# A two-layer token mixer with experts: modulations per 128 columns, rows and weight loads around the second layer's gather, gate-row products of a tile pair in one group

## The chip, the cores and the metric

One core of a Trainium2 chip runs the kernel. The metric is device time in microseconds of one execution; the three runs shown took 2120.23, 2123.27 and 2123.53 us, median 2123.27.

## What is computed

A backbone of two layers works on 512 latent tokens and 256 context tokens of width 1024, all in float32. Each layer normalises the rows, scales and shifts them by modulations (six vectors of 1024 per layer, made by a product of a condition vector with a 1024 x 6144 matrix), mixes the tokens, adds the result, normalises again and sends the rows through 16 experts. The first layer's mixer joins gated linear attention and a gated linear recurrence; the second is a bidirectional matrix memory. Cut to what matters here:

```python
mods = split(silu(c) @ mod_w[layer] + mod_b[layer], 6)        # sh1 sc1 g1 sh2 sc2 g2
xn = rmsnorm(x, norm1_g[layer]) * (1 + sc1) + sh1
y = mixer(xn)                  # layer 0: xn @ ab_w_in (2592 columns), scans, @ ab_w_out
                               # layer 1: xn @ m_w_up (4096 columns), q/k/v, gates, memory, @ m_w_down
x = x + g1 * y
t = rmsnorm(x, norm2_g[layer]) * (1 + sc2) + sh2
probs = softmax(t @ router_w[layer])
gate, idx = top_k(probs.T, 2 * tokens // 16)                  # each expert chooses its tokens
xe = t[idx]
ye = (silu(xe @ w_gate) * (xe @ w_up)) @ w_down * gate
x = x + g2 * scatter_add(idx, ye)
gates(d) = concat(q, k, v) @ w_gates[d] + b_gates[d]          # layer 1: 16 rows of gates in all
```

Every expert has three 1024 x 1024 matrices, so each layer's experts read 16 x 12 MB of weights.

## The kernel before, in words

The program is written as Python that emits instructions; the framework's planner then sets the order of the instructions on each engine by a simulated timeline. Three means bind it: program order, which gives the priority; a raised priority for the splitting of weights (`high_priority`, line 338); and `issue_after(x)`, which queues the instructions of a block behind `x` on the same engine. TensorE, VectorE, ScalarE, GpSimd (POOL) and SyncE (SP) each work through their own queue in order.

**Weights and slots.** Weights come in pieces of 1 MB into slots of 8 KB per partition (`slot`, line 79), which are handed out in a fixed cycle; a load waits until its slot's last reader is done. In the first layer's mixer the cycle has four slots, and both the weights of the projections (`load_cols`, line 101) and those of the modulations (`load_rows`, line 114) take them in program order, so that each load stands four places behind the one whose slot it takes. All of these loads are issued from SyncE's queue.

**Projections.** `proj_tiles` (line 365) loads 256 columns of a weight, and yields the product for each 128 of them (`proj`: the weights are split into a high and a low part, and 48 products of each 128 columns are added in one PSUM tile). After each 256 columns it calls `fill_step` (line 217).

**Modulations.** `mod_block` (line 172) is a generator for one block of 1024 columns in two halves. A half loads two slots, makes the products with 32 columns of the condition (line 182, four row groups at 32-partition offsets), copies the result, and yields; the next call transposes it back by small products (line 190), adds the bias (line 193) and goes on with the next half. `fill_step` takes one such step. The first layer's list (line 411) has six blocks, so twelve steps with products and a thirteenth that only finishes. Steps run at the places where `fill_step` is called: in `proj_tiles`, and twice behind each of the two column halves of the value projection (lines 460 to 482). What is left over runs at line 522, ahead of a branch (line 528) that chooses between two forms of the linear attention, at which the engines meet. In the second layer the list holds steps made on VectorE (`mod_steps`, line 225).

**The second layer's up projection.** For each 128 columns, `up_tile` (line 1481) makes a convolution, a block-diagonal product and `gx`, two 128 x 32 factors. For each pair of such tiles the gate rows are made by four products per column range (lines 1523 to 1530): two factors times the tile before its convolution or after it, each into its own 32 partitions of a PSUM tile, for 512 latent and 256 context columns; VectorE adds the sum to `gacc`.

**The way into the second layer's experts.** After the memory, `down` (line 1563) makes the down projection in two halves of 512 columns; the first half's result is multiplied by the modulation `G` and added to the residual (lines 1608 to 1614). `route_end` (line 1075) scales the rows and writes them to memory for the gather (lines 1105 to 1108, buffers `xt`, written by GpSimd's queue to `xh_d`), finds each expert's tokens by eight rounds of maxima, and writes the indices `gidx` (line 1158). `experts` (line 1166) then gathers the first expert's rows (`fetch`, line 1183, an indirect DMA on GpSimd's queue), transposes them (line 1207), and makes for each expert the gate, up and down products (line 1252).

Weights for the first two experts are sent ahead (lines 1278 to 1280): 22 slots in the pools `r1` (3), `r2` (6), the ring (4), `r3` (7) and `ry` (2), in the order gate weights of expert 0, all from its third up piece on, and at last its first two up pieces (`first`, line 1632). The first three loads are queued behind marks in the memory, the others behind a load of the down projection, all on SyncE. The pool `r3` lies where the memory's tiles were, `ry` where the routing's tiles are (`Br`, freed by the writes of `xh_d`). From the second expert on, each load takes the slot of a weight that has been used.

Of the kernel before, what the change touches and what calls it, by code (L numbers as in the profile page):

```python
# [9 lines left out]
F32 = mybir.dt.float32  # L10
# [5 lines left out]
ALU = mybir.AluOpType  # L16
# [4 lines left out]
P = 128  # L21
D = 1024
# [26 lines left out]
class Backbone:  # L49
# [81 lines left out]
    def setup(self):  # L131
        nc, cp, I = self.nc, self.cp, self.I
        self.cols = cp.tile([P, NCOL], F32, name="cols")
        nc.scalar.dma_start(self.cols, I["cols"])
        self.ident = cp.tile([P, P], F32, name="ident")
        make_identity(nc, self.ident)

        self.sT = cp.tile([P, 8, 32], F32, name="sT")
        nc.vector.memset(self.sT, 0.0)
        for v, nme in enumerate(("c", "c_ctx")):  # L140
            nc.scalar.activation(self.sT[:, :, v], self.col(nme, 0, 8), AF.Silu)

        self.modc = cp.tile([P, 2, 6, 8, 2], F32, name="modc")
        self.g_d = self.dr.tile([2, 2, 8, 2, P], F32, name="g_d")
        self.mhalf = cp.tile([P, 1], F32, name="mhalf")
        nc.vector.memset(self.mhalf, -0.5)
        self.one = cp.tile([P, 1], F32, name="one")
        nc.vector.memset(self.one, 1.0)

        self.pick = cp.tile([P, 2], F32, name="pick")  # L150
        nc.vector.tensor_reduce(
            self.pick, self.ident.rearrange("p (g r) -> p r g", g=4)[:, :2, :], AX.X, ALU.add
        )

        self.copy = cp.tile([P, 2], F32, name="copy")
        for v, n in enumerate((2, 4)):
            for i in range(n):
                nc.vector.memset(self.copy[i * (P // n) : (i + 1) * (P // n), v : v + 1], float(i))
        self.fill = []
        self.eps = cp.tile([P, 1], F32, name="eps")  # L160
        nc.vector.memset(self.eps, EPS)
        self.gla_limit = GLA_LIMIT
        E = mybir.EngineType
        self.flag_engines = [E.PE, E.Activation, E.DVE, E.Pool]
        self.rw = cp.tile([P, 2, KC, NE], F32, name="rw")
        nc.scalar.dma_start(self.rw, I["rw"])
        self.xh_d = [self.dr.tile([n, D], F32, name=f"xh{v}_d") for v, n in enumerate((TL, TC))]
        self.xa_d = [self.dr.tile([n, D], F32, name=f"xa{v}_d") for v, n in enumerate((TL, TC))]
        self.ss = cp.tile([P, NT, 2], F32, name="ss")
# [195 lines left out]
    def proj_tiles(self, pool, w2d, c0, n, ctx=True):  # L365

        for c in range(c0, c0 + n, 256):
            w = self.load_cols(w2d, c, min(256, c0 + n - c))
            for j in range(0, min(256, c0 + n - c), P):
                yield self.proj(pool, w[:, :, j : j + P], P, ctx)  # L370
            self.fill_step()

    def apply_T(self, lhs, rhs, M=P):

# [6 lines left out]
    def layer0(self):  # L381
        tc, nc, I = self.tc, self.nc, self.I
# [11 lines left out]
        with ExitStack() as sx:  # L394
            px = op("A_x", sx)
# [47 lines left out]
        with ExitStack() as sr:  # L443
            prg = op("A_rg", sr)
            bd = prg.tile([P, 8, P], F32, name="bd")
            nc.gpsimd.memset(bd, 0.0)
            xb = [xb_[:, j, :] for j in range(4)]
            for j, pw in enumerate(self.proj_tiles(big, w_in, 2080, 512)):
                xr = prg.tile([P, T], F32, tag="rt", name=self.nm("xr"), bufs=4)
                nc.scalar.copy(xr, pw[:, TC:])  # L450
                self.conv(xb[j], xr, "rg_cw", 4, j, "rg_cb")
            self.rg_pair(prg, 0, xb, bd, sps, h)
            nc.vector.tensor_copy(lr, self.proj32(self.load_cols(w_in, 1536, 32))[:, TC:])
            for j, pw in enumerate(self.proj_tiles(big, w_in, 0, 256)):
                nc.scalar.mul(q[:, j, :], pw[:, TC:], 0.125)
            for j, pw in enumerate(self.proj_tiles(big, w_in, 256, 256)):
                nc.scalar.copy(k[:, j, :], pw[:, TC:])
            last = self.rg_pair(prg, 1, xb, bd, sps, h)

            for c in range(2):  # L460
                w = self.load_cols(w_in, 512 + 256 * c, 256)
                wp = []
                for hf in range(2):
                    wp.append([big.tile([P, 4, 256], F32R, tag=t_, name=self.nm("wv"), bufs=2) for t_ in ("wh", "wl")])
                    with tc.high_priority(offset=HP):
                        self.split(*wp[hf], w[:, 4 * hf : 4 * hf + 4, :], True)
                pw = [self.pW() for _ in range(2)]
                acc = [pw[t // 2][:, 512 * (t % 2) : 512 * (t % 2) + 256] for t in range(4)]
                acc += [self.pT()[:, :256] for _ in range(2)]
                for hf in range(2):  # L470
                    for t in range(NT):
                        i, x0 = (1, t) if t < 2 else (0, t - 2)
                        for kk in range(4 * hf, 4 * hf + 4):
                            wh, wl = (a[:, kk % 4, :] for a in wp[hf])
                            for n, (a, b) in enumerate(((self.xh, wh), (self.xh, wl), (self.xl, wh))):
                                nc.tensor.matmul(
                                    acc[t], a[i][:, kk, ts(x0, P)], b, start=kk == 0 and n == 0, stop=kk == KC - 1 and n == 2
                                )
                        if hf:
                            nc.scalar.copy(v[:, t, ts(c, 256)], acc[t])  # L480
                self.fill_step()
                self.fill_step()
        o = big.tile([P, 4, T], F32, tag="o", name="o_gla")
        with ExitStack() as sg:
            pg = op("A_gla", sg)
# [156 lines left out]
        sb = ExitStack()  # L642
# [432 lines left out]
    def route_end(self, R, small, mid=None):  # L1075
# [27 lines left out]
        last = nc.scalar.activation(pr, pr, AF.Exp)  # L1103
        with self.tc.issue_after(last.ins):
            for t in range(t0, t0 + nt):
                xt = pool.tile([P, D], F32, tag="xt", name=self.nm("xt"), bufs=2)
                nc.scalar.mul(xt, self.xt(t), rs[:, t - t0 : t - t0 + 1])
                nc.gpsimd.dma_start(self.xh_d[v][ts(t - t0, P), :], xt)
        nc.vector.tensor_reduce(sm, pr, AX.X, ALU.add)
# [56 lines left out]
    def experts(self, layer, has_ctx, px, queued=None, once=None):  # L1166
# [66 lines left out]
        def load(n, eng=None):  # L1233
            e, n = divmod(n, 12)
            return self.load_pairs(W[n // 4][e], 256 * (n % 4), eng)
# [39 lines left out]
        if has_ctx:  # L1275
            queue = [(5, nc.sync, None), (8, nc.gpsimd, self.fetched[0]), (12, nc.gpsimd, self.fetched[1])]
        else:
            for n, l in enumerate(once[1]):
                with self.tc.issue_after((self.marks + [queued] * 22)[n].ins):
                    ahead[l] = load(l)  # L1280
            self.set_ring(*once[2])
            queue = []
        xeT = expand(xe, regions[:1])
# [140 lines left out]
    def layer1(self):  # L1424
# [93 lines left out]
        for j, pu in enumerate(up):  # L1518
            pr.append((j, *up_tile(pu, j)))
            if j % 2 == 0:  # L1520
                continue

            for c0, n in ((TC, TL), (0, TC)):
                pg = self.pT()
                for g in range(4):
                    jj, xm, gx = pr[g // 2]
                    src = xm[:, c0 : c0 + n] if g % 2 else (xc, xk)[c0 == 0][jj]
                    nc.tensor.matmul(
                        pg[32 * g : 32 * g + 32, :n], gx[:, g % 2, :], src, start=True, stop=True
                    )  # L1530
                if j == 1:
                    nc.vector.tensor_copy(gacc[:, c0 : c0 + n], pg[:, :n])
                else:
                    nc.vector.tensor_tensor(gacc[:, c0 : c0 + n], gacc[:, c0 : c0 + n], pg[:, :n], ALU.add)
            pr = []
# [60 lines left out]
        with tc.tile_pool(name="C_dn", bufs=1, side="right", reuse_waits="tile") as pd:  # L1596
            G = self.mod_rows(pd, 1, 2, 1)
            for nh in range(2):
# [8 lines left out]
                        queued = self.loaded  # L1607
                for t in range(4):
                    xs = self.xt(2 + t)[:, ts(nh, 512)]
                    y = acc[t]  # L1610
                    if nh == 0:
                        y = pd.tile([P, 512], F32, tag="y", name=self.nm("y"), bufs=2)
                        nc.vector.tensor_tensor(y, acc[t], G[:, 0, :512], ALU.mult)
                    nc.vector.tensor_tensor(xs, xs, y, ALU.add)
                if nh == 0:
                    w = [self.pW(), self.pW()]
                    R = self.route_open(1, 0, pr, w[0][:, :512])
# [6 lines left out]
        self.psum_moe()  # L1624
        sr.close()
        sb = ExitStack()
        r3 = self.weight_ring(sb, 7, "right")
        px = self.pool(self.sb, "Bx", 2, "left")
        sy = ExitStack()
        ry = self.weight_ring(sy, 2, "left")  # L1630
        self.set_ring(r1, r2, self.ring, r3, ry)
        first = [*range(4), *range(6, 22), 4, 5]
        self.experts(1, False, px, queued, (sy, first, (r1, r2, self.ring, r3)))
        sy.close()
        self.moe_close()
        s2.close()
# [358 lines left out]
```

## Time and profile before

| | |
|---|---|
| median of 3 runs | 2123.27 us |
| profiled execution | 2123.27 us |
| its span, first to last instruction | 2121.6 us |
| mean granted TensorE clock | 0.976 |
| TensorE matmul busy | 1974.9 us (93%) |
| VectorE busy | 881.8 us (42%) |
| ScalarE busy | 570.6 us (27%) |
| GpSimd busy | 234.9 us (11%) |
| bytes moved | 587.06 MB, mean 277 GB/s |

The stages follow each other: the first layer's mixer until about 360 us, its output projection and routing until 470, its experts until 1030, the second layer's up projection until 1300, the memory until 1540, down projection and routing until 1645, and the second layer's experts to the end. The shares of busy time are means over these stages and say little of any one of them. A granted clock of 1.00 is 2.4 GHz, 0.50 is 1.2 GHz.

### The profile page before, as it was taken

The page shows a single profiled execution, that of the slowest core. Times are in us where ns is not written, and L with a number is a line of the kernel's source. Part 1 is how long each engine was busy: PE and PEld are TensorE (multiplying, and loading weights), DVE is VectorE, ACT ScalarE, POOL GpSimd, SP SyncE. Part 2 cuts the span into 40 slices and gives each one's busy share as a digit, 9 for nine tenths or more (in the row PEclk, how much of TensorE's full clock was granted, in tenths as well). Part 3 has the DMA queues.
Part 4 walks back from the last instruction along what each step waited for, and adds up shares of the span by engine and source line. Part 5 has one row for each costly group of instructions (what it writes and reads, how often), then busy time and mean ns, then how long its engine had stood idle before and what let it go on. Part 6 is the DMA issues. An engine that isn't in the chain of part 4 may idle for free. (4 is left out here: it accounts for less than half of the span.)

```text
span 2121.6 us, 30206 instructions
## 1 busy us (share of the span) xinstructions
PE 1974.9 (93%) x12346; PEld 1180.4 (56%) x12346; DVE 881.8 (42%) x1765; ACT 570.6 (27%) x1009; POOL 234.9 (11%) x286
## 2 busy tenths in 40 slices
PE   6998997989999999999999999999996799998886
PEld 4676775763444444444678867888875233333322
DVE  3654673561101111021777766467675132222223
ACT  3365442520000000011533435455433000000001
POOL 1000100211111111110000012311140000000000
PEclk8998997999999999999999999999998899999999
DMA  8443523548999999999455555433846899999997
GB/s 303 131 143 100 181 82 103 200 172 326 411 403 404 410 401 411 404 414 377 148 180 183 186 180 166 158 124 110 292 194 238 307 419 420 420 420 419 420 420 289
DMA packets 188303, 587.06 MB, mean 277 GB/s; under 512 B 15304, under 2 KB 84984, under 8 KB 139008
## 3 DMA queue, kind: packets, MB, share of 16 engines
q1 hardware_dynamic: 172816, 546.50, 66.7%
q0 software_dynamic: 11168, 33.46, 4.9%
q10 hardware_dynamic: 4176, 5.11, 0.7%
q8 instruction: 100, 1.64, 0.3%
q14 instruction: 43, 0.35, 0.0%
HBM read 544.60 MB, written 40.42 MB: 276 GB/s over the span
## 5 line engine op out<-in xcount | busy, mean ns | idle before, releaser
L1252 PE MATMUL L<-w,xeT 128*64 128x512 f32 x2048 | 476.1, 600 | 21.4 <-DMA w<-in_exp_w_gate_dram 10.8
L1252 PEld LDWEIGHTS L<-w,xeT 128*64 128x64 f32 x2048 | 145.0, 137 | 322.8 <-issue 261.9
L1252 PE MATMUL L<-w,hL 128*64 128x512 f32 x1024 | 228.3, 596 | 16.7 <-ACT hL L1328 11.8
L1309 DVE TENSOR_TENSOR sgl<-sgl,L 128x512 f32<-128x512 f32 x32 | 22.0, 689 | 365.1 <-PE L L1252 364.3
L1252 PEld LDWEIGHTS L<-w,hL 128*64 128x64 f32 x1024 | 70.0, 137 | 152.0 <-issue 121.1
L1265 PE MATMUL C<-w,xeT 128*32 128x256 f32 x2048 | 116.9, 380 | 1.3 <-DVE xeT L1214 1.3
L1303 ACT ACTIVATE sgl<-L 128x512 f32<-128x512 f32 x32 | 19.1, 598 | 347.6 <-PE L L1252 347.6
L1328 ACT COPY hL<-T 128x512 f32<-128x512 f32 x32 | 18.8, 586 | 335.0 <-PE T L1326 335.0
L276 DVE TENSOR_TENSOR wl<-w,wh 128x1024 fp32r<-128x1024 f32 (+1 forms) x80 | 86.6, 1084 | 40.1 <-ACT wh L274 39.5
L345 PE MATMUL W<-xhl,wl 128*128 128x512 f32 x256 | 102.0, 398 | 1.3 <-DVE wl L276 1.3
L345 PE MATMUL W<-xhl,wh 128*128 128x512 f32 x256 | 103.0, 402 | 0.0
L345 PE MATMUL W<-xll,wh 128*128 128x512 f32 x256 | 101.7, 397 | 0.0
L1183 POOL DMA_INDIRECT xe<-xh_d,gidxL x32 | 31.5, 984 | 633.5 <-PE T L1207 629.6
L1265 PEld LDWEIGHTS C<-w,xeT 128*32 128x32 f32 x2048 | 64.2, 110 | 63.6 <-issue 25.8
L345 PE MATMUL W<-x,wh 128*128 128x512 f32 x256 | 96.4, 399 | 0.6 <-ACT y L324 0.6
L1419 DVE TENSOR_TENSOR X<-X,T 128x512 f32<-128x512 f32 x76 | 48.0, 683 | 95.4 <-PE T L1417 95.3
L274 ACT CAST wh<-w 128x1024 fp32r<-128x1024 f32 (+1 forms) x64 | 53.1, 831 | 112.0 <-PE W L347 71.4
L347 PE MATMUL W<-x,wh 128*128 128x256 f32 x256 | 72.2, 282 | 0.0
L1369 DVE SCALAR_TENSOR_TENSOR y<-L,gateL,G 64x512 f32<-64x512 f32 x32 | 24.0, 750 | 115.3 <-PE L L1252 114.8
L1840 PE MATMUL T<-w,Ah 128*128 128x512 f32 x192 | 62.1, 401 | 1.4 <-ACT Ah L274 1.4
L1372 ACT CAST yL<-y 64x512 fp32r<-64x512 f32 x36 | 22.2, 617 | 150.5 <-DVE y L1369 134.6
L1265 PE MATMUL C<-w,hC 128*32 128x256 f32 x1024 | 58.6, 380 | 0.0
(514 smaller groups left out, 3580.4 us busy)
## 6 DMA issues: line engine op xcount, KB each, us to landing
w<-in_exp_w_gate_dram SPq DMA_DIRECT2D x128, 1024.0 KB, 20.5
w<-in_exp_w_up_dram SPq DMA_DIRECT2D x125, 1024.0 KB, 20.1
w<-in_exp_w_down_dram SPq DMA_DIRECT2D x124, 1024.0 KB, 20.1
w<-in_mod_w_dram SPq DMA_DIRECT2D x48, 1024.0 KB, 5.6
w<-in_m_w_up_dram SPq DMA_DIRECT2D x16, 1024.0 KB, 5.9
w<-in_ab_w_in_dram SPq DMA_DIRECT2D x10, 1024.0 KB, 5.2
w<-in_m_w_down_dram SPq DMA_DIRECT2D x8, 1024.0 KB, 10.0
vh_d<-vth SPq DMA_DIRECT2D x16, 384.0 KB, 3.0
```

The source lines that it names most:

```text
L274: i = (nc.vector.tensor_copy if vector else nc.scalar.copy)(hi, src)
L276: return i, nc.vector.tensor_tensor(lo, src, hi.bitcast(F32), ALU.subtract)
L345: nc.tensor.matmul(pw[:M, 512:], a[:, k, :M], b[0][:, k, :], **st)
L347: nc.tensor.matmul(pw[:M, 256:512], a[:, k, :M], b[1][:, k, :], **st)
L1183: self.fetched.append(nc.gpsimd.indirect_dma_start(out=xe[v], out_offset=None, in_=self.xh_d[v][:, :].rearrange("t (h c) -> (t h) c", c=w) ...
L1252: last = nc.tensor.matmul(L[64 * h : 64 * h + 64, :], a, w[k_ // 2][:, k_ % 2, ts(h, 512)], start=k_ == 0, stop=k_ == KC - 1,)
L1265: last = nc.tensor.matmul(C[32 * h : 32 * h + 32, :], b, w[k_ // 2][:, k_ % 2, ts(h, 256)], start=k_ == 0, stop=k_ == KC - 1,)
L1309: nc.vector.tensor_tensor(sgl, sgl, ul, ALU.mult)
L1369: nc.vector.scalar_tensor_tensor(y32[ph, :], dl[ph, :], gL[ph, e : e + 1], G[ph, 0, ts(h, 512)], ALU.mult, ALU.mult)
L1372: nc.scalar.copy(hi, y32[ph, :])
L1419: nc.vector.tensor_tensor(xs, xs, ps, ALU.add)
L1840: nc.tensor.matmul(O, x_[:, s, :], y_[s], start=s == 0 and m == 0, stop=s == NT - 1 and m == 2)
```

## The change

1. In the first layer, `fill_step` is called after every 128 columns instead of every 256, until the second recurrence pair has been emitted (`often`); behind each half of the value projection one step is left instead of two.
2. In the second layer the buffers of scaled rows (`xt`) are four instead of two.
3. Of the 22 loads sent ahead, the last three (a down piece of the second expert and the first two up pieces of the first) go on GpSimd's queue behind the first gather, instead of SyncE's. The seventh slot of `r3` becomes a pool of its own, `r4`.
4. The four products of gate rows of a tile pair are chained by `issue_after`, the younger tile's first.
5. In the down projection's first half the product with `G` is written back into PSUM instead of into a tile `y`, which is gone.

```diff
@@ setup
         self.fill = []
+        self.often = True
@@ proj_tiles
             for j in range(0, min(256, c0 + n - c), P):
                 yield self.proj(pool, w[:, :, j : j + P], P, ctx)
-            self.fill_step()
+                if self.often or j:
+                    self.fill_step()
@@ layer0
             last = self.rg_pair(prg, 1, xb, bd, sps, h)
+            self.often = False
...
                             nc.scalar.copy(v[:, t, ts(c, 256)], acc[t])
                 self.fill_step()
-                self.fill_step()
@@ route_end
-                xt = pool.tile([P, D], F32, tag="xt", name=self.nm("xt"), bufs=2)
+                xt = pool.tile([P, D], F32, tag="xt", name=self.nm("xt"), bufs=(2, 4)[layer])
@@ experts
             for n, l in enumerate(once[1]):
-                with self.tc.issue_after((self.marks + [queued] * 22)[n].ins):
-                    ahead[l] = load(l)
+                if n < 19:
+                    with self.tc.issue_after((self.marks + [queued] * 19)[n].ins):
+                        ahead[l] = load(l)
+                else:
+                    with self.tc.issue_after(self.fetched[0].ins):
+                        ahead[l] = load(l, nc.gpsimd)
@@ layer1
+            lead = None
             for c0, n in ((TC, TL), (0, TC)):
                 pg = self.pT()
-                for g in range(4):
+                for g in (2, 3, 0, 1):
                     jj, xm, gx = pr[g // 2]
                     src = xm[:, c0 : c0 + n] if g % 2 else (xc, xk)[c0 == 0][jj]
-                    nc.tensor.matmul(
-                        pg[32 * g : 32 * g + 32, :n], gx[:, g % 2, :], src, start=True, stop=True
-                    )
+                    with tc.issue_after(lead.ins) if lead else nullcontext():
+                        lead = nc.tensor.matmul(
+                            pg[32 * g : 32 * g + 32, :n], gx[:, g % 2, :], src, start=True, stop=True
+                        )
...
                     xs = self.xt(2 + t)[:, ts(nh, 512)]
-                    y = acc[t]
                     if nh == 0:
-                        y = pd.tile([P, 512], F32, tag="y", name=self.nm("y"), bufs=2)
-                        nc.vector.tensor_tensor(y, acc[t], G[:, 0, :512], ALU.mult)
-                    nc.vector.tensor_tensor(xs, xs, y, ALU.add)
+                        nc.vector.tensor_tensor(acc[t], acc[t], G[:, 0, :512], ALU.mult)
+                    nc.vector.tensor_tensor(xs, xs, acc[t], ALU.add)
...
-        r3 = self.weight_ring(sb, 7, "right")
+        r3 = self.weight_ring(sb, 6, "right")
+        r4 = self.weight_ring(sb, 1, "right")
...
-        self.set_ring(r1, r2, self.ring, r3, ry)
+        self.set_ring(r1, r2, self.ring, r3, r4, ry)
         first = [*range(4), *range(6, 22), 4, 5]
-        self.experts(1, False, px, queued, (sy, first, (r1, r2, self.ring, r3)))
+        self.experts(1, False, px, queued, (sy, first, (r1, r2, self.ring, r3, r4)))
```

## Rows read from the trace of the kernel before

**Rows 1.** Chain of waits: the second layer's first gather (start us, us, what).

```profile
1645.39 7.43 DMA xe<-xh_d,gidxL
```

**Rows 2.** Timeline of SyncE from 1655 us: the 23rd load of the last experts.

```profile
1659.29 2.35 SPq L111 DMA_DIRECT2D w<-in_exp_w_down_dram  x2
```

**Rows 3.** Windows: busy us of each engine (instructions), granted clock, DMA share, GB/s.

```profile
core 0: us, PE busy (x) PEld busy (x) DVE busy (x) ACT busy (x) POOL busy (x), PEclk, DMA share, GB/s
58.00:149.00 91.00, 91.00 (x530) 66.27 (x527) 56.47 (x102) 42.77 (x56) 0.00 (x0) 1.00 0.36 112
...
182.00:198.00 16.00, 9.86 (x67) 5.33 (x66) 13.39 (x17) 6.69 (x10) 0.00 (x0) 0.81 0.76 254
...
353.00:361.00 8.00, 6.80 (x34) 3.42 (x33) 0.34 (x2) 0.85 (x2) 0.00 (x0) 0.61 0.34 106
...
1070.00:1256.00 186.00, 186.00 (x1141) 147.24 (x1139) 135.02 (x270) 72.55 (x133) 5.36 (x17) 1.00 0.58 186
...
1652.00:1659.30 7.30, 4.83 (x14) 1.97 (x16) 1.38 (x2) 0.00 (x0) 0.97 (x1) 0.50 0.14 40
...
1845.00:2100.00 255.00, 224.54 (x953) 77.74 (x950) 60.95 (x93) 20.05 (x34) 6.61 (x7) 1.00 1.01 418
```

**Rows 4.** Timeline of TensorE in the value projection (idle time before and releaser in brackets).

```profile
170.57 1.60 PE L476 MATMUL W<-wv,x 128*128 128x256 f32 x12
...
176.41 2.93 PE L476 MATMUL W<-wv,x 128*128 128x256 f32 x12 [3.65 <-ACT v L480]
...
182.32 0.99 PE L190 MATMUL T<-pick,mr 128*128 128x2 f32 x8
183.25 1.93 PE L182 MATMUL T<-w,sT 128*32 128x512 f32 x16
187.88 1.26 PE L190 MATMUL T<-pick,mr 128*128 128x2 f32 x8 [2.70 <-ACT mr L186]
189.06 3.35 PE L182 MATMUL T<-w,sT 128*32 128x512 f32 x16
...
197.59 1.65 PE L476 MATMUL W<-wv,x 128*128 128x256 f32 x6 [3.40 <-DVE wv L276]
```

**Rows 5.** Timeline of SyncE from 170 to 199 us: the second half's value weights.

```profile
184.37 0.37 SPq L105 DMA_DIRECT2D w<-in_ab_w_in_dram  x1
```

**Rows 6.** Timeline of TensorE around the branch.

```profile
353.31 1.87 PE L190 MATMUL T<-pick,mr 128*128 128x2 f32 x8
...
368.55 2.07 PE L995 MATMUL T<-sq,ones 128*128 128x512 f32 x2 [8.04 <-ACT sq L992]
```

**Rows 7.** The page's part 6: modulation loads, KB of one, us to landing.

```profile
w<-in_mod_w_dram SPq DMA_DIRECT2D x48, 1024.0 KB, 5.6
```

**Rows 8.** Timeline of TensorE: eight gate-row passes, from their first to what follows.

```profile
1095.73 0.62 PE L1528 MATMUL T<-xc,gx 128*32 128x512 f32 x1
...
1097.14 0.39 PE L347 MATMUL W<-xhc,wl 128*128 128x256 f32 x1
```

**Rows 9.** Windows of the gate-row line alone: PE and weight loads, clock, DMA.

```profile
1070.00:1256.00 186.00, 25.35 (x128) 5.24 (x128) 1.00 0.58 186
```

**Rows 10.** Timeline of GpSimd ahead of the second layer's gather.

```profile
1637.94 0.54 POOL L1108 DMA_DIRECT2D xh_d<-xt  x1 [8.86 <-ACT xt L1107]
...
1645.39 1.06 POOL L1183 DMA_INDIRECT xe<-xh_d,gidxL  x1 [3.17 <-DMA xh_d<-xt]
```

**Rows 11.** Timeline of VectorE: the indices.

```profile
1641.98 0.18 DVE L1158 SCALAR_TENSOR_TENSOR gidxL<-d,gi 128x16 uint32<-128x16 f32 x1
```

**Rows 12.** Timeline of GpSimd in the first layer: weight loads behind the second gather.

```profile
466.43 1.69 POOL L111 DMA_DIRECT2D w<-in_exp_w_up_dram  x3
```

**Rows 13.** Instructions on xe from 462 to 467 us: the gather ahead of those loads.

```profile
DMA to landing us min/median/max: 3.7/3.7/3.7
```

**Rows 14.** Line 1614: minimum, median and maximum ns, operand in SBUF (y) and PSUM (T).

```profile
L1614 DVE TENSOR_TENSOR X<-X,y x4: 680/1186/1770, 1562.6 to 1573.3; 128x512 f32<-128x512 f32 x4
L1614 DVE TENSOR_TENSOR X<-X,T x4: 679/680/689, 1616.3 to 1618.1; 128x512 f32<-128x512 f32 x4
```

**Rows 15.** Timeline of TensorE at the end of the down projection's first half.

```profile
1569.38 0.50 PE L1582 MATMUL T<-wl,mh 128*128 128x512 f32 x1 [2.36 <-DVE wl L276]
```

## The prediction

> **What bounds the kernel now.** I read the windows first, for which engine is full where; then the chain of waits; then the timelines of the three places that the change touches. In the projections of both layers TensorE has no hole: 91.00 of 91 us in the first layer's stretch from 58 to 149 us, 186.00 of 186 us in the second layer's up projection, where VectorE has 135 us and the DMA engines half of their time [rows 3]. Time taken off TensorE there is time off the path. The last 255 us are of another kind: the DMA engines are full (share 1.01, 418 GB/s) and TensorE waits for them [rows 3], and the chain that ended last is there a string of weight loads, one behind the other. The end of the kernel is therefore the time at which the second layer's stream of weights starts to flow without a break, and the bytes still to come. Just ahead of it the DMA engines lie almost idle for 7.3 us (share 0.14, [rows 3]): 22 loads have been sent ahead, all ring slots are full, and the 23rd goes out at 1659.29, when the first expert's first products have freed the first slot [rows 2]. Those products wait for the token gather, which took 7.43 us [rows 1]. So every microsecond by which the gather ends earlier is one off the end, and so is every one saved before it, as everything behind is placed by what it waits for.
>
> **Part 1, the modulations.** There are twelve steps with products and loads (six blocks of two halves) and one that only finishes. By the code the old order runs 4 of them up to the keys, 4 in the value projection, 2 with the output gates, 1 with the GELU gates, and the last two behind everything. The new one puts 8 up to the keys, 2 in the value projection, 2 with the output gates, and the one without products with the GELU gates. A step that meets no wait costs 0.99 + 1.93 us less their overlap, 2.9 us [rows 4].
> *Taken out.* Between the value projection's two column halves TensorE needs from 182.32 to 197.59, 15.3 us, for two steps and the finish of a third, with waits of 2.70 and 3.40 us, and the second step's products take 3.35 instead of 1.93 us [rows 4]; the clock granted over this stretch was 0.81, partly at 1.2 instead of 2.4 GHz behind those waits [rows 3]. The second half's weights are sent for only at 184.37 [rows 5], since with four ring slots that load stands four places behind the step's first load and takes its slot. In the new order one step lies between, and the load stands behind a slot that was free long before: 15.3 - 2.9 = 12.4 us. One step less behind the second half: 2.9. The products of the step in the GELU gates: 1.9. The two steps behind everything: from 353.31 to 360.51 (where the wait of 8.04 us begins), 7.2 us, 1.87 us where 0.99 is usual [rows 4, 6] (granted clock 0.61, so mostly 1.2 GHz, [rows 3]), and only then does the branch let the next stage start [rows 6]; without them about 6.9 of it go, the rest being the last copy, which is needed anyway. Together 24.1.
> *Put in.* Four more steps in the stretch from 58 to 149, which is full: 4 x 2.9 = 11.6. Their loads find the DMA engines at a share of 0.36 [rows 3]; what hides them is the projection of 128 columns in front of each step, 48 products of on average 0.163 us (186 us for 1141 in the up projection, [rows 3]) or 7.8 us, against 5.6 us for a modulation load [rows 7]. SyncE's queue carries the same loads in another order.
> Net 24.1 - 11.6 = **12.5 us**. Ends: nothing, if the holes in the value projection come back in another place; 17.5, if also the wait of 3.65 us at 176.41 for ScalarE's copies and the half clock behind it (the next 12 products took 2.93 us, the 12 before the wait 1.60) disappear [rows 4].
>
> **Part 2, the gate rows.** Today the products of a tile pair run two abreast: eight passes (two products, two column ranges, two passes each) fill 1.41 us from 1095.73 to 1097.14 [rows 8], and there are 128 passes, 25.35 us in all [rows 9]. The modulation products with the same 32-column form run four abreast: 16 passes in 1.93 us [rows 4], half of the price of a pass. In one group the 16 x 1.41 = 22.6 us become 11.3, so **11.3 us** fall on an engine that is full. Ends: 12.7, half of the busy time, and nothing, if the four don't meet. The chain of issue only orders products that are all ready with the younger tile's factors; behind it on TensorE stand projection products with nothing to wait for but their own weights.
>
> **Part 3, rows, loads and gather.** With two buffers the third scaled row tile waits 8.86 us for the first one's write to land, and the gather is released by the fourth write at 1645.39 [rows 10]; the indices are there from 1642.16 on [rows 11]. With four buffers the third and fourth writes go out without that wait. The gather can start between 1642.2 (indices) and 1645.4 (as now); I take 1642.7, near the index, because the writes that end last go out some 8 us earlier. Its duration: 7.43 us now, with two weight loads sent out just ahead of it; in the first layer a gather with three weight loads directly behind it on GpSimd's queue [rows 12] landed in 3.7 us [rows 13]. I take 3.7; ends 3.7 and 7.43. The gather then ends at 1646.4 instead of 1652.8: **6.4 us** (ends 0 and 7.0). The three loads now behind it cost GpSimd 1.69 us of issue [rows 12], ahead of the second gather, which waits for the first's transposes anyway. At 418 GB/s they need 7.5 us and fill the hole; two of them carry the first expert's up weights and should be there by some 1654, while its gate products run. The SyncE queue loses three loads, of which the last two stood waiting for the routing pool.
> The Trainium skill (Trainium Kernel Development and Optimization, Key Constraints) says that transfers issued from SP, ACT and POOL share the same 16 engines and interleave, so that another issuing engine alone saves issue time; by that the gather keeps its neighbours, and this part gives only the earlier start. The first layer's 3.7 us speaks against it.
>
> **Part 4, the product in place.** The four additions read the residual and a product in SBUF at 1.19 us (median), beside GpSimd's multiplications; with one operand in PSUM they took 0.68 [rows 14]. Four times 0.51 is 2.0 us of VectorE, where TensorE waits 2.36 us for a split queued behind them [rows 15]. On the other side the PSUM tile comes free one addition later, 0.7 us. I take **1.4 us**; ends -0.7 and 2.0.
> The Trainium skill (VectorE: DVE Perf Modes, The TRN2 errata) charges a PSUM operand 62 cycles more per instruction than an SBUF one. By it this part would lose some 0.3 us (an estimate, four additions); the row, taken at another time, says that it wins.
>
> **The sum.** 12.5 + 11.3 + 6.4 + 1.4 = 31.6 us. The profiled execution took 2123.27 us itself (span 2121.6), which is also the median of the three runs, so the forecast is 2123.3 - 31.6 = **2091.7 us**.
>
> **The rivals.** (a) *The modulations give nothing:* the ring of four slots puts the next weight load behind two pairs of modulation loads instead of one, and what TensorE gains later it waits for earlier. For it: the old value projection stalled in just this way [rows 4, 5]. Against it: a projection of 7.8 us now lies between two steps. 2123.3 - 19.1 = 2104.2 us; chance 0.15. (b) *The four products don't meet*, because the planner sets others between or PSUM is late: 2123.3 - 20.3 = 2103.0; chance 0.06. (c) *The gather keeps its 7.43 us*, sharing the engines with the three loads: only 2.7 of part 3 is left, 2095.4; chance 0.13. (d) *Slower:* each of the eight early steps waits on TensorE for its own load, which can be sent only when the ring turns. 8 x 5.6 = 45 us [rows 7] on top of the forecast gives 2091.7 + 45 = 2136.7. It decides once such waits pass the 31.6 us that the rest brings, nearly six full landings of the eight. Against it: no wait for a load stands in the four early steps now, in a stretch that is full [rows 3]. Chance 0.05. (e) *Little is left:* the parts work, but the path before the gather turns out to end elsewhere; about 2121, chance 0.02.
>
> **The numbers.** The forecast case has 0.59. Its own bounds reach down to 2123.3 - (17.5 + 12.7 + 7.0 + 2.0) = 2084.1; (a) and (b) lie at 2103 to 2104, and a little of (c) on top of (a) at 2108. I give 2083 to 2107, with a microsecond below the bounds for the clock elsewhere. About 0.2% (4.2 us) is what a measurement here can tell from no change. Faster: all but (d), (e) and a remainder of 0.01, 0.92; same 0.03; slower 0.05.
>
> **What would show it.** Right: no load of value weights waits behind a modulation step, no TensorE hole of 2 to 4 us between the value projection's halves, no modulation product behind the last linear-attention copy; gate-row products starting in fours within 0.05 us and eight passes in about 0.95 us; a pair of up tiles 1.4 us shorter; four row writes within some 4 us, the gather landing in under 4 us, no DMA hole before the 23rd load. Wrong: new TensorE holes before 149 us that wait for a modulation or weight load; a gather that still takes 7 us, or products of the first expert that wait for its up weights; a last stretch that is no longer full of DMA.

## The result, and the profile after

The changed kernel takes 2099.64 us (median of 4 runs, 2096.33 to 2102.32), the kernel before 2123.4 in the same session (4 runs): ratio 0.9886, 95% interval 0.9872 to 0.99, 23.8 us less. The forecast was 31.6 us less, at 2091.7 us; the measured time lies within its range. The profiled execution took 2099.13 us, its span 2097.4. Read from the timelines, stage by stage, in us (the last column, also as the difference from the kernel before, belongs to the best experiment, described below; a stage ends with the event named, the fifth with ScalarE's first instruction for the squares):

| stage, up to | before | changed | difference | forecast | both remedies |
|---|---|---|---|---|---|
| first projection product | 49.96 | 48.53 | -1.4 | 0 | -0.3 |
| last copy of the keys | 96.35 | 112.89 | +16.5 | +11.6 | +11.8 |
| last value product | 70.36 | 55.61 | -14.8 | -15.3 | -15.0 |
| last copy of the linear attention | 137.01 | 140.66 | +3.7 | -1.9 | +3.5 |
| first square behind the branch | 12.67 | 1.03 | -11.6 | -6.9 | -11.7 |
| first expert product, layer 0 | 104.63 | 109.34 | +4.7 | 0 | -1.8 |
| first up-projection product, layer 1 | 573.98 | 575.10 | +1.1 | 0 | +1.4 |
| first down product | 461.69 | 444.89 | -16.8 | -11.3 | -16.4 |
| last down product | 111.03 | 111.00 | 0.0 | -1.4 | -1.0 |
| gather issued | 27.72 | 25.38 | -2.3 | -2.7 | -2.2 |
| first expert product, layer 1 | 10.18 | 6.25 | -3.9 | -3.7 | -3.9 |
| end | 466.00 | 466.72 | +0.7 | 0 | +0.5 |

Rows two to six are part 1: forecast -12.5, measured -1.5. Parts 2 and 3 came as forecast or better. Small differences in one row need care: up to the first projection product, where no part does anything, the thirteen profiles of this case lie between 46.75 and 50.65 us. Where part 1 went is seen at three places. First, TensorE at the seventh of the eight early steps (start, duration, what; idle time before it and its releaser in brackets):

```profile
151.67 0.30 PE L213 MATMUL T<-ident,modc 128*16 128x128 f32 x1 [2.83 <-DVE modc L194]
151.91 3.54 PE L183 MATMUL T<-w,sT 128*32 128x512 f32 x16
```

The step that follows block 2's second half begins with the transposition of that block's gate, and this waits 2.83 us for a sum queued on VectorE; the next 16 products take 3.54 us where the pattern of [rows 4] has 1.93 (granted clock 0.55 from 151.67 to 155.50). Second, the windows of the linear attention's last blocks (columns as in [rows 3]):

```profile
334.00:346.00 12.00, 10.31 (x60) 8.06 (x59) 8.64 (x20) 6.11 (x14) 0.00 (x0) 0.73 0.26 88
346.00:358.00 12.00, 11.39 (x37) 8.55 (x36) 2.02 (x6) 1.60 (x6) 0.00 (x0) 0.50 0.02 4
```

The granted clock is already 0.73 in the first of them; before it was 0.98 there. TensorE's rows, of the changed kernel and then of the kernel before, show where it fell:

```profile
338.69 0.71 PE L834 MATMUL W<-qt,kt 64*128 64x128 f32 x8 [0.84 <-ACT gl L509]
339.56 1.22 PE L834 MATMUL W<-qt,kt 64*128 64x128 f32 x8 [0.16 <-PE W L834]
```

```profile
342.57 0.71 PE L832 MATMUL W<-qt,kt 64*128 64x128 f32 x8 [1.12 <-DVE A L839]
345.09 0.79 PE L847 MATMUL T<-qh,st 64*128 64x128 f32 x4
346.54 1.22 PE L847 MATMUL T<-qh,st 64*128 64x128 f32 x4
```

Groups of products that take 0.71 us at full speed take 1.22 at half speed (1.2 GHz): from 339.56 on in the changed kernel, from some 345 on before. The gaps alone do not tell why: before, longer ones (1.17 us at 338.17, 1.12 at 342.57) stood ahead of the fall. The last five blocks run from 338.69 to the last copy at 357.69, 19.0 us; before, from 338.17 to 353.68, 15.5. Third, behind the branch: VectorE, then TensorE, then GpSimd.

```profile
392.09 1.23 DVE L277 TENSOR_TENSOR wo<-w,wo 128x1024 fp32r<-128x1024 f32 x1 [1.52 <-ACT wo L275]
398.19 1.29 DVE L587 TENSOR_TENSOR y_ab<-L,G 128x512 f32<-128x512 f32 x2 [4.88 <-DMA G<-g_d]
```

```profile
396.70 2.43 PE L571 MATMUL C<-wo,x 128*128 128x512 f32 x10
400.14 1.35 PE L1064 MATMUL L<-ident,X 128*128 128x128 f32 x8 [1.01 <-DVE X L588]
402.54 0.75 PE L1064 MATMUL L<-ident,X 128*128 128x128 f32 x4 [1.05 <-DVE X L588]
404.81 1.13 PE L1064 MATMUL L<-ident,X 128*128 128x128 f32 x4 [1.53 <-DVE x L1067]
407.01 2.74 PE L1072 MATMUL T<-x,rws 128*32 128x128 f32 x16 [1.07 <-ACT x L1069]
```

```profile
386.86 3.98 POOL L1049 TENSOR_TENSOR rws<-rw,modc 128x128 f32<-128x128 f32 x1
390.78 1.84 POOL L258 DMA_DIRECT2D G<-g_d  x2
```

TensorE began on what follows the branch 9.7 us earlier than before (358.85, not 368.55, [rows 6]), but VectorE, which multiplies its result by the gates `G`, waited 4.88 us for them to land, and TensorE then stood 4.66 us in four gaps. The load of `G` stands on GpSimd's queue behind a product of 3.98 us. In the kernel before such a wait hid:

```profile
403.97 1.29 DVE L585 TENSOR_TENSOR y_ab<-L,G 128x512 f32<-128x512 f32 x2 [0.96 <-DMA G<-g_d]
```

TensorE had output products until 408.67 there, so nothing was lost by it.

The gate rows, TensorE's timeline (these answer to [rows 8]; the first row is the last projection product, the last what follows the group):

```profile
1166.48 0.40 PE L346 MATMUL W<-xhl,wh 128*128 128x512 f32 x1
1166.81 0.62 PE L1537 MATMUL T<-xc,gx 128*32 128x512 f32 x1
1166.81 0.62 PE L1537 MATMUL T<-xm,gx 128*32 128x512 f32 x1
1166.82 0.62 PE L1537 MATMUL T<-xc,gx 128*32 128x512 f32 x1
1166.83 0.62 PE L1537 MATMUL T<-xm,gx 128*32 128x512 f32 x1
...
1168.23 1.10 PE L244 MATMUL T<-one,ma 128*128 128x1 f32 x8
```

Four start within 0.02 us, and the sixteen take 1.42 us (1166.81 to 1168.23). Line 1537 is busy for 11.98 us, not 25.35 [rows 9]. The way into the second layer's experts, on GpSimd, on TensorE, and the window behind it ([rows 10, 1, 3]):

```profile
1608.89 0.64 POOL L1110 DMA_DIRECT2D xh_d<-xt  x1 [5.82 <-ACT xt L1109]
...
1612.00 0.53 POOL L1110 DMA_DIRECT2D xh_d<-xt  x1 [0.51 <-ACT xt L1109]
1624.43 1.07 POOL L1185 DMA_INDIRECT xe<-xh_d,gidxL  x1 [11.90 <-DVE tokL L1164]
1625.51 0.61 POOL L111 DMA_DIRECT2D w<-in_exp_w_down_dram  x1
1626.07 1.11 POOL L111 DMA_DIRECT2D w<-in_exp_w_up_dram  x2
```

```profile
1628.07 1.10 PE L1209 MATMUL T<-ident,xe 128*128 128x128 f32 x4 [5.61 <-DMA xe<-xh_d,gidxL]
```

```profile
1628.00:1634.50 6.50, 4.92 (x14) 1.96 (x16) 1.38 (x2) 0.00 (x0) 1.02 (x1) 0.50 1.01 420
```

The four writes lie within 3.1 us, the gather waits for VectorE and no longer for a write, its first transposition runs 3.64 us after its issue, and the DMA engines are full at once (share 1.01, where 0.14 stood); SyncE sends the 23rd load at 1634.40, not 1659.29 [rows 2].

### The profile page after: what moved, and what is told of

Read it like the earlier page. It is cut to its first block, busy times and chain, and to the rows that moved or that the text cites. A ratio compares the mean times of both kernels' runs of the same rounds, so it can differ in the third digit from the quotient of the medians.

```text
span 2097.4 us, 30199 instructions
## 1 busy us (share of the span) xinstructions
PE 1963.6 (94%) x12346; PEld 1182.1 (56%) x12346; DVE 879.5 (42%) x1765; ACT 571.0 (27%) x1009; POOL 238.2 (11%) x289
## 4 chain that ended last, share of the span: by engine, by line
PE 59%; DMA 13%; DVE 4%; issue 2%; ACT 1%; POOL 1%; SPq 0%; DVEq 0%; POOLq 0%; ACTq 0%
PE L L1254 24%; PE C L1267 8%; PE W L346 6%; DMA w<-in_exp_w_gate_dram 5%; DMA w<-in_exp_w_down_dram 4%; PE T L1848 3%; DMA w<-in_exp_w_up_dram 3%; PE W L348 2%; PE T L1591 2%; PE W L1796 2%; PE T L1516 1%; PE W L1591 1%; PE T L1424 1%; PE W L1797 1%; PE T L1333 1%
## 5 line engine op out<-in xcount | busy, mean ns | idle before, releaser
L346 PEld LDWEIGHTS W<-x,wh 128*128 128x128 f32 x256 | 48.0, 188 | 21.3 <-issue 4.7
```

Of the source, the lines that this page charges most:

```text
L346: nc.tensor.matmul(pw[:M, 512:], a[:, k, :M], b[0][:, k, :], **st)
```

## The experiments

Theory at the start: every part as measured stage by stage above. Rival: the sum on record, part by part. Ratios are to the kernel before, run in the same session (medians there 2125.21, 2124.85 and 2127.54 us).

**Part 1 alone.**

```diff
@@ the kernel before
+        self.often = True
...
-            self.fill_step()
+                if self.often or j:
+                    self.fill_step()
...
+            self.often = False
...
-                self.fill_step()
```

> The kernel before with the modulation steps alone moved (a step per 128 columns in the first layer's early projections, one less per half of the value projection). Theory A (the sum of the prediction: all of part 1 arrives): 12.5 us less, 2110.9 us, and the first expert product of the first layer 12 us earlier than 470.98. Theory B (from the trace of the changed kernel: the early steps cost 15 us ahead of the value projection, not 11.6, and 217 to 468 us gets longer again): 2 to 6 us less, 2117 to 2121 us; a TensorE gap of some 2.8 us near 152 us in front of the transposition of block 2's gate row, and the first expert product 3 to 5 us earlier than 470.98.

2124.29 us, ratio 0.9992 (0.9982 to 1.0002): no difference that the runs can tell, and at most 4 us less, so not theory A and at best the lower end of theory B. In the profile (of the slowest of the eleven runs) the first expert product came at 469.63, 1.35 us earlier; the gap of theory B stood in its place:

```profile
152.26 0.28 PE L213 MATMUL T<-ident,modc 128*16 128x128 f32 x1 [2.46 <-DVE modc L194]
```

**Part 2 alone.**

```diff
@@ the kernel before
-                for g in range(4):
+                for g in (2, 3, 0, 1):
...
+                    with tc.issue_after(lead.ins) if lead else nullcontext():
```

> The kernel before with the chained gate rows alone. Theory A (the sum: 11.3 us from the products themselves): 2112.1 us, a pair of tiles 1.4 us shorter (25.75 to 24.3). Theory B (from the trace of the changed kernel: each interruption of the up projection that is left out gives some 0.4 us more than its products' own time): 14 to 17 us less, 2106 to 2110 us, a pair 23.8 us.

2106.9 us, ratio 0.9918 (0.9905 to 0.9931): 17.4 us less, more than the sum's 11.3, and a pair takes 23.84 us: theory B. The profiled run is the slowest of the five, and its profile shows 12.1 us less up to the first down product (449.60 for 461.69). Up to the end of the last gate rows it is 14.4 us shorter than before (196.69 for 211.10 us), as the changed kernel is (196.65); behind them, from 1342.66 to 1367.66 in the memory, it ran at a granted clock of 0.86, where the kernel before and the changed kernel have 1.00 all the way.

**Parts 3 and 4.** The four buffers take the space that the product in place frees, so part 3 was not tried without part 4, nor its buffers apart from its loads.

```diff
@@ the kernel before
+                xt = pool.tile([P, D], F32, tag="xt", name=self.nm("xt"), bufs=(2, 4)[layer])
...
+                    with self.tc.issue_after(self.fetched[0].ins):
+                        ahead[l] = load(l, nc.gpsimd)
...
+                        nc.vector.tensor_tensor(acc[t], acc[t], G[:, 0, :512], ALU.mult)
```

> The kernel before with four buffers for the rows, three loads on GpSimd's queue behind the gather, and the product in place, whose freed buffers the rows need. Theory A (the sum: 6.4 + 1.4): 7.8 us less, 2115.6 us. Theory B (in place gives nothing, the rest comes as summed): 6.3 us less, 2117.1 us, gather landed in some 3.6 us after its issue in place of 7.43, and issued 2.4 us earlier against the last down product. Rival C (the gather keeps its 7.43 us): 2.7 us less, 2120.7 us.

2114.19 us, ratio 0.9952 (0.994 to 0.9963): 10.2 us less; the profile's stages from the first down product to the first expert product sum to 8.0 us less, near theory A's 7.8. The gather's transposition ran 3.61 us after its issue: rival C falls.

**Part 4 alone.**

```diff
@@ the kernel before
-                        nc.vector.tensor_tensor(y, acc[t], G[:, 0, :512], ALU.mult)
-                    nc.vector.tensor_tensor(xs, xs, y, ALU.add)
+                        nc.vector.tensor_tensor(acc[t], acc[t], G[:, 0, :512], ALU.mult)
+                    nc.vector.tensor_tensor(xs, xs, acc[t], ALU.add)
```

> The kernel before with the gated product in place alone. Theory A (the sum): 1.4 us less, 2122.0 us, the down projection from its first to its last product 1.4 us shorter than 111.0. Theory B (from the changed kernel, whose down projection took 111.0 as well): no difference, 2123.4 us within 1 us; VectorE's sum into X falls from about 1.2 us to 0.7, but TensorE's clock falls in its place.

2122.87 us, ratio 0.9992 (0.998 to 1.0004): too small for the runs to tell. In the profile the down projection took 109.21 us, 1.8 less, with TensorE's waits cut from 1.21 and 2.36 us to 0.33 and 1.26, and the clock at 1.00 behind them:

```profile
1565.90:1577.90 12.00, 12.00 (x60) 9.42 (x59) 9.18 (x12) 6.00 (x14) 5.45 (x4) 1.00 0.26 89
```

In the changed kernel the same window reads:

```profile
1548.10:1560.10 12.00, 12.00 (x54) 9.55 (x54) 8.36 (x12) 6.08 (x13) 4.10 (x3) 0.87 0.23 74
```

TensorE is as busy, at a granted clock of 0.87, and much the same waits (0.33, 1.63) stand ahead of it. One profile of each is too little here, so all thirteen were read. At a granted clock of 1.00 the down projection took 110.2 to 111.1 us in the three programs without part 4 and 109.2 to 110.5 in the four with it. Where the clock fell to 0.86 to 0.88 for 12 us, it took 112.3 in the one without part 4 (part 1 alone) and 110.6 to 111.6 in the five with it. By the means of these groups part 4 is worth about 1.0 us at either clock and the fall costs about 1.5 (estimates). The clock fell with part 4 and without it; what makes it fall is open.

**The changed kernel without part 1** (the first experiment's edit, undone there).

> The changed kernel with its modulation steps put back where they were before. Theory A (part 1 gives next to nothing in company too, as alone): 2100.5 us, within 2 us of the changed kernel's 2099.64. Theory B (the gains measured one by one add up without it: 17.4 and 10.2 us from 2123.4): 2095.8 us, so that part 1 costs some 4 us in the changed kernel. Theory C (the sum of the prediction, 12.5 us): 2112.1 us.

2098.41 us, ratio 0.9885 (0.9867 to 0.9904), the changed kernel's own: theory A, though the interval just reaches theory B's 0.987; theory C falls. The first expert product comes 419.05 us after the first projection product, in the changed kernel 419.53. Part 1 is worth nothing that the runs or the profiles can tell, alone or in company.

**The gates' load on another queue.**

```diff
@@ the changed kernel, mod_rows and its call
-            self.nc.gpsimd.dma_start(
+            (eng or self.nc.gpsimd).dma_start(
...
-        G = self.mod_rows(big, 0, 2, tag="o", shape=[P, 4, T])
+        G = self.mod_rows(big, 0, 2, tag="o", shape=[P, 4, T], eng=nc.sync)
```

> The changed kernel with the first layer's gate rows G loaded on SyncE's queue in place of GpSimd's, where a product of 3.98 us stands ahead of them. Theory A (behind the branch the chain to G sets the end, so an earlier branch gives nothing): G issued at 387 us and not 390.8, landed near 394.5 and not 398.1, TensorE's four gaps from 400 to 407 us (4.66 us together) shrink to about 1, and the time is 3.5 us less, 2096.1 us. Theory B (VectorE's own work, or the loads of the experts behind it, sets the end): the first expert product stays at 468 us, or the time at 2099.6 us.

2091.57 us, ratio 0.9849 (0.9828 to 0.987): 8.1 us less than the changed kernel (7.9 by the ratios), more than theory A's 3.5. SyncE, VectorE and TensorE:

```profile
384.77 1.00 SPq L258 DMA_DIRECT2D G<-g_d  x2
```

```profile
391.66 1.23 DVE L277 TENSOR_TENSOR wo<-w,wo 128x1024 fp32r<-128x1024 f32 x1 [3.52 <-ACT wo L275]
392.81 1.28 DVE L587 TENSOR_TENSOR y_ab<-L,G 128x512 f32<-128x512 f32 x2
```

```profile
395.82 2.89 PE L571 MATMUL C<-wo,x 128*128 128x512 f32 x12
398.55 1.59 PE L1064 MATMUL L<-ident,X 128*128 128x128 f32 x12
400.44 0.74 PE L1064 MATMUL L<-ident,X 128*128 128x128 f32 x4 [0.30 <-DVE x L1067]
```

VectorE multiplies 5.4 us earlier with no wait for `G`, of the four gaps 0.51 us are left (0.30 and 0.21), and the granted clock from 398.7 to 411.7 us is 1.00 where the changed kernel has 0.74 from 399 to 412. The first expert product comes at 460.15, 7.9 us earlier, and 7.3 of it reach the end of the profile.

**Another order of the blocks.**

```diff
@@ the changed kernel
-        self.fill = [self.mod_block(0, b) for b in (3, 4, 2, 5)] + [self.mod_block(1, b) for b in (1, 0)]
+        self.fill = [self.mod_block(l, b) for l, b in ((0, 3), (0, 4), (1, 1), (1, 0), (0, 2), (0, 5))]
```

> The changed kernel with the modulation blocks in another order: the two with a transposition and rows to memory (blocks 2 and 5 of the first layer) last. Theory A (the wait of 2.8 us for VectorE in front of block 2's transposition, and the half clock behind it, are lost time): the last key copy at 157 us and not 161.4, 4.5 us less at the end, 2095 us. Theory B (another chain, VectorE's recurrences and decays, sets when the linear attention ends): its last copy stays at 357.7 us within 1 us and the time at 2099.6 us.

2096.05 us, ratio 0.9856 (0.9835 to 0.9877), an interval that overlaps the changed kernel's. The early stage shrank by 4.8 us (112.89 to 108.11) and the linear attention's last copy came at 352.35 (1.8 of these 5.3 us are an earlier first product), so theory B falls there. But VectorE then waited 4.20 us for `G`, TensorE's four gaps were 4.36 us, and from the first projection to the first expert product only 1.3 us were left.

**One step later.**

```diff
@@ the changed kernel, behind each half of the value projection
-                self.fill_step()
```

> The changed kernel without the one step that was left in each half of the value projection, so that two steps come later, one of them between the products of the last gate projection. Theory A (the linear attention's last five blocks take 18.7 us in place of 15.2 because TensorE's clock fell to half at 339 us and not at 345, for want of the steps that stood ahead of them): those blocks take about 15.2 us again, the rest of the last step costs 2 us ahead of the branch, the time is 1 to 2 us less, 2098 us. Theory B (the blocks wait for VectorE, whatever the clock): 18.7 us stay, and the time is 2101 to 2102 us.

2101.03 us, ratio 0.9887 (0.9868 to 0.9905). The last five blocks ran from 337.19 to the last copy at 352.84, 15.7 us instead of 19.0, with the clock up in the first window, as theory A has it:

```profile
334.00:346.00 12.00, 9.38 (x66) 7.19 (x67) 9.04 (x24) 5.42 (x14) 0.00 (x0) 0.93 0.00 0
```

The time went against theory A: a whole step, and not a remainder of 2 us, was left ahead of the branch, and the stage up to the first square was 12.87 us again.

**Both remedies:** the order and the load together.

> The changed kernel with both: blocks 2 and 5 last, and G on SyncE's queue. Theory A (the 4.5 us that the order gained ahead of the branch were lost again in the wait for G only): 4 to 5 us less than with G on SyncE alone (2091.57), 2087 us. Theory B (the order is worth what it showed at the first expert product, 1.3 us): 2090.3 us.

2091.8 us against 2127.54, ratio 0.9829 (0.9816 to 0.9842): below the changed kernel's interval, and the best ratio of all; on 2123.4 us it would be 2087. Its interval overlaps that of the load alone. The profiles are 3.9 us apart at the first expert product (407.78 and 411.70 us after the first projection product), so theory A holds in the trace, and the runs do not settle it. No wait stands ahead of the early steps any more.

**The load without part 1,** in the changed kernel and in the kernel before.

> G on SyncE's queue and everything else of the change, but the modulation steps where they were before. Theory A (part 1 brings the branch some 6 us forward, and only the wait for G kept that from the end): 5 to 6 us more than with the steps moved (2091.57), 2097 us. Theory B (part 1 is worth nothing even then, because the products that stood in the holes have to be done somewhere): 2091.6 us within 1.5 us.

2103.61 us, ratio 0.9891 (0.9876 to 0.9905). With `G` on SyncE the modulation steps are worth 0.9891 - 0.9849 = 0.0042, 9 us; with `G` on GpSimd 0.9885 - 0.9886, nothing: theory A, and somewhat more than its 5 to 6 us (the two intervals, up to 0.987 and from 0.9876, do not overlap, if barely). The profiles agree: the first expert product comes 419.62 us after the first projection product without the moved steps and 411.69 with them, 7.9 us apart.

> The kernel before with G on SyncE's queue and nothing else. Theory A (there the branch is late and TensorE has products of the output projection left until G is there: nothing waits for it): no difference, 2124 us within 1.5 us. Theory B (the products behind G's rows set the end with or without the change): some 5 us less or more, 2119 us.

2125.05 us, ratio 0.999 (0.998 to 1.0001): theory A. There VectorE multiplied right behind its own split, and TensorE was still full, so the load's queue does not matter:

```profile
402.69 1.22 DVE L276 TENSOR_TENSOR wo<-w,wo 128x1024 fp32r<-128x1024 f32 x1 [3.85 <-ACT wo L274]
403.83 1.28 DVE L585 TENSOR_TENSOR y_ab<-L,G 128x512 f32<-128x512 f32 x2
```

## Why the prediction was right, and where it was wrong

The time lies within the range, but the forecast itself was missed by 7.9 us, and that it was not missed by more is luck: part 1 brought 11 us too little, and part 2 up to 5.5 us more than its sum held.

**Part 1** is where it failed, by 11 us. What was to be taken out went: the holes between the value projection's halves (-14.8 for -15.3) and the steps ahead of the branch (-11.6 for -6.9). The 4.7 us beyond the forecast are TensorE's part of the branch, whose wait the prediction left standing (sequencer rows, duration in ns, start in us; before, then changed):

```profile
L528 PEldq COMPARE_BRANCH  x1: 6098/6098/6098, 360.1 to 360.1; - x1
L530 PEldq COMPARE_BRANCH  x1: 4800/4800/4800, 353.7 to 353.7; - x1
```

Before, its 6.10 us stand behind the last modulation products; in the changed kernel its 4.80 us lie beside products that go on until 357.39. Three steps failed. "Net 24.1 - 11.6" took the earlier branch as a gain at the end and asked of nothing behind it what would be late next: it was the load of `G`, 4.66 us of gaps, with a granted clock of 0.74 from 399 to 412 us, where the kernel before has 1.00 from 404 to 416; the stage grew by 4.7 us. That the load decided is shown by the four combinations of load and steps: the steps are worth 9 us with the load moved, nothing without. "Four more steps ... 4 x 2.9 = 11.6" looked only at loads and products; the finish of block 2 waits for VectorE, 2.83 us, and a clock of 0.55 follows: 16.5 in place of 11.6, and with the other order 11.8. And the products "of the step in the GELU gates" were to save 1.9 us; in their place the clock fell earlier, at 339 us instead of 345, and the stage grew by 3.7, which the step moved back there undid. With both remedies rows two to six give 13.2 us in the profile: the 12.5 were there to be had, but only with two edits that the prediction did not have. Rival (a), nothing from the modulations, came true in its result with another mechanism than the ring of slots.

**Part 2** was put too small: 16.8 us by the profile, 17.4 alone by the runs, for 11.3. The direct term was about right: 25 runs of gate rows occupied 23.75 us, now 8 occupy 11.42, so 12.3. The rest of a pair's 1.91 us (25.75 to 23.84) is 0.37 us per pair; with it go two of three interruptions. The price of one is seen in the kernel before:

```profile
1177.29 0.59 PE L1528 MATMUL T<-xc,gx 128*32 128x512 f32 x1
1177.30 0.59 PE L1528 MATMUL T<-xm,gx 128*32 128x512 f32 x1
1177.82 0.51 PE L345 MATMUL W<-xhl,wh 128*128 128x512 f32 x1
1178.25 0.40 PE L1528 MATMUL T<-xk,gx 128*32 128x256 f32 x1
```

A lone projection product between two gate-row passes stretches 0.43 us (1177.29 to the next pass in [rows 8], 1096.18 to 1096.61) and 0.24 us (its usual spacing) to 0.96, 0.3 us more; the same 0.96 stand in seven of the eight pairs. The Trainium skill (TensorEngine Tiling (Array Packing), Key Properties) says that a change of the tiling mode drains TensorE. These 0.3 us fit that; that they are the drain no run shows. Of the 16.8 us, 14.4 lie ahead of the end of the gate rows, the same with part 2 alone. The other 2.3 lie between the gate rows and the down projection (250.58 to 248.24 us); with part 2 alone that stretch took 252.91, so they are not shown to be part 2's.

**Part 3** was right in both terms: issue -2.3 for -2.7, landing -3.9 for -3.7. Rival (c) is out: the gather's rows were in use 3.64 us after its issue, not 7.43. In the kernel before two weight loads went out at 1644.72, just ahead of the gather, and the DMA engines' share was 0.91 from 1645.40 to 1648.00 and 0.84 from there to 1652.80; in the changed kernel it was 0.49 from 1624.40 to 1628.00. The price has moved: the second gather, at 1629.80 and now behind the three loads, landed in 7.9 us, where it took 3.4 before. Its rows are first used at 1650.35, so nothing waits for it. That the loads' place is the cause, and not the earlier writes, is argued from these rows; no run has the one without the other. The Trainium skill (Trainium Kernel Development and Optimization, Key Constraints) says that transfers issued from several engines interleave on the same 16 DMA engines, and that another issuing engine saves issue time only. The second gather's 7.9 us agrees; what the prediction drew from it, that the first gather keeps its neighbours, did not hold, because the loads were also put behind it.

**Part 4** was right in its sign and near in its size: -1.8 us in the down projection by one profile, about -1.0 by the groups of profiles, forecast -1.4. In the changed kernel's profile the granted clock of 0.87 took it back. The four additions take 0.67 us with their operand in PSUM; with both operands in SBUF the fastest took 0.68 and the median 1.19 [rows 14]. The Trainium skill (VectorE: DVE Perf Modes, The TRN2 errata) puts 62 cycles on a PSUM operand; no such loss is seen here.

The rival of full landings in front of the early steps, 2136.7 us, did not come: the steps wait for no load.

## What to carry to other kernels

When work is moved so that a stage starts earlier, list what that stage needs that does not start earlier with it, loads on a busy engine's queue above all: here one small load behind a 4 us product kept a gain of 8 to 9 us from the end, and changing its queue was worth nothing before the change. A step is not only its products: its finish on another engine, queued behind long work there, holds the engine that waits for it. And a part measured at zero may be a part whose gain is waiting behind something else, so measure it again with the suspect removed.

## What was not expected of the hardware

Products of TensorE taken out ahead of a stretch with gaps went with an earlier fall of its clock: with a step less ahead of them, five blocks of linear attention took 19.0 us instead of 15.5, the granted clock 0.73 in place of 0.98 in the same window, and a step put back undid it. In the down projection the granted clock fell to 0.86 to 0.88 for 12 us in six of thirteen profiles, with the shorter wait and without it. A lone full product between two runs of 32-column products cost 0.3 us more than its usual spacing. And TensorE's branch instruction, 6.1 us behind the last products, cost next to nothing where products went on beside it.
